# Scores of two heads at a time, with the high parts on two halves of the array's rows

## The chip, the core and the metric

The kernel runs on one core of a Trainium2 chip. The metric is the device time of one execution in microseconds (us). TensorE does the matrix products, VectorE (DVE) and ScalarE (ACT) the elementwise work, GpSimd (POOL) some small operations, and SyncE (SP) issues most of the transfers (DMA). PEld in the profile is TensorE's loading of the stationary operand ("weights"), which can overlap a running matmul. A matmul takes its stationary operand from SBUF as rows x columns, streams the moving operand through the array, and writes to PSUM, which the kernel uses as eight banks.

## The reference

Two layers of a decoder trunk on 512 positions of width 1024. Each layer is half a SwiGLU, a mixer, and another half SwiGLU. The mixer runs three kinds of attention from one input projection:

```python
for layer in range(DEPTH):                                   # DEPTH = 2
    x = x + 0.5 * swiglu(rmsnorm(x, g0), ...)
    x = x + hybrid_mixer(rmsnorm(x, g1), ...)
    x = x + 0.5 * swiglu(rmsnorm(x, g2), ...)

# in hybrid_mixer, heads of 64, causal, 512 positions
logits = einsum('bqhd,bsd->bqhs', qi, ki)                    # 8 index heads, one key
iscore = einsum('bqhs,bqh->bqs', relu(logits), wi)           # the top 128 keys of it are A's mask
sc_a = einsum('bqhd,bkd->bhqk', qa, ka) * scale              # 4 heads, one key head
sc_b = einsum('bqhd,bkhd->bhqk', qb, kb) * scale             # 4 heads
sc_c = einsum('bqhcd,bshcd->bhcqs', qc, kc) * scale          # 4 heads with 2 maps each
```

Each score goes through a masked softmax and is multiplied with the values.

## The kernel before

Values are float32. A product is kept exact enough by splitting each operand into a high part that the array takes in one pass (`F32R`) and a low part, the rest; `mm3` (L227 to L229) then makes a dense product of three passes (high x low, high x high, low x high).

Attention's scores use that a head has only 64 dimensions. `to_heads` splits the projected tile of a block of 128 positions into high and low (ACT at L819, DVE at L820), and the array transposes it head by head (L826), so that a head's tile has the 64 high rows on partitions 0 to 63 and the 64 low rows on 64 to 127. `swapped` makes a copy of a key tile with the halves exchanged, by two transfers from SP's queue. `scores` then takes two full passes for one head and one block `i` of 128 queries against the `(i + 1) * 128` keys so far: with the swapped keys (L844: high x low and low x high in one pass, the cross products), and with the keys as they are (L845: high x high and low x low). The moving operand is therefore 128, 256, 384 or 512 columns wide. The result goes to one of three PSUM banks with the tag `sc`, which the dense products of `product` use too.

Scores are made in `index_scores` (8 heads, i = 1 to 3), `attend` for B and for A (heads in pairs, i = 0 to 3; A has one key head for all) and `attend_c` (two maps of each head). Each is a generator. The loop at the end of `mixer` takes from it a step or two for each step of dense work (six dense matmuls, or a product), so that score passes stand in TensorE's queue between dense ones. `behind` ties them to the last dense matmul that was recorded, and a scheduler then settles the order. After the softmax, weights are transposed (L867) and multiplied with the values: L879 for C, and L892 in `weighted_pair` for A and B, which writes the two heads of a pair to the two halves of the output's partitions (so each matmul has 64 of the array's columns).

The feed-forward stages run before and after each mixer and contain no scores.

Of the kernel before, what the change touches and what calls it, by code (L numbers as in the profile page):

```python
# [13 lines left out]
F32 = mybir.dt.float32  # L14
# [3 lines left out]
AF = mybir.ActivationFunctionType  # L18
ALU = mybir.AluOpType
AX = mybir.AxisListType  # L20

P = 128
# [7 lines left out]
HD = 64  # L30
# [49 lines left out]
def trunk_kernel(ctx, tc, xt_in, pos_in, ng_in, wgu, wdn, wgrp, wgate, wbr_s, wbr_c, wo, qkg_in, lam_in, subg_in, out):  # L80
    nc = tc.nc
    V, S, G, PE = nc.vector, nc.scalar, nc.gpsimd, nc.tensor
# [12 lines left out]
    def nm(s):  # L95
        _n[0] += 1
        return f"{s}_{_n[0]}"

    def bank(tag="mm"):
        return ps.tile([P, 512], F32, tag=tag, name=nm(tag), bufs=BANKS[tag])  # L100

    def slot(dt=F32, tag="h", cols=512):
        return big.tile([P, cols], dt, tag=tag, name=nm(tag), bufs=SLOTS)

    def temp(tag, dt=F32, cols=512, bufs=2):
        return (phase[-1] if tag in ("p0", "p1", "pt", "e", "u") else tmp).tile([P, cols], dt, tag=tag, name=nm(tag), bufs=bufs)
# [622 lines left out]
    def mixer(l, n, nxt, aside):  # L729
# [71 lines left out]
        def defer(steps, fn):  # L801

            late.append([steps, fn])
# [9 lines left out]

        def to_heads(v, nh, t, dst, lag, done):

            s = phase[-1].tile([P, 8, 2, HD], F32R, tag="st", name=nm("st"), bufs=ST)

            def split():
                S.activation(s[:, :nh, 0, :], v[:, :nh], AF.Copy)  # L819
                V.tensor_tensor(s[:, :nh, 1, :], v[:, :nh], s[:, :nh, 0, :].bitcast(F32), op=ALU.subtract)  # L820
                defer(LAG_H, turn)

            def turn():
                ps_ = [bank("tr") for _ in range(0, nh, 4)]
                for h in range(nh):
                    PE.transpose(ps_[h // 4][:, h % 4 * P:(h % 4 + 1) * P].bitcast(F32R),  # L826
                                 s[:, h].rearrange("p a d -> p (a d)"), ident_r)
                for h in sorted(range(nh), key=lambda h: (h % 4, h)):
                    nc.any.tensor_copy(dst[h][:, t * P:(t + 1) * P], ps_[h // 4][:, h % 4 * P:(h % 4 + 1) * P])
                done[0] += 1  # L830

            defer(lag, split)

        def swapped(src):
            d = slot(F32R)
            nc.sync.dma_start(d[:HD, :].bitcast(F32), src[HD:, :].bitcast(F32))
            nc.sync.dma_start(d[HD:, :].bitcast(F32), src[:HD, :].bitcast(F32))
            return d

        def scores(q, k1, k2, i):  # L840

            o = bank("sc")[:, :(i + 1) * P]
            ql = q[:, i * P:(i + 1) * P]
            PE.matmul(o, ql, k2[:, :(i + 1) * P], start=True, stop=False)  # L844
            PE.matmul(o, ql, k1[:, :(i + 1) * P], start=False, stop=True)  # L845
            return o

        def softmax_parts(q, k1, k2, i, mask, tag):

            o = scores(q, k1, k2, i)  # L850
            w = (i + 1) * P
            mx = sm.tile([P, 1], F32, name=nm("mx"), tag="mx", bufs=4)
            pr = temp(tag, bufs={"p0": P0, "p1": P1}[tag])
            V.tensor_tensor_reduce(out=pr[:, :w], in0=o, in1=mask, scale=-1.0, scalar=-TAKEN,
                                   op0=ALU.add, op1=ALU.min, accum_out=mx)
            den = sm.tile([P, 1], F32, name=nm("den"), tag="den", bufs=4)
            S.activation(pr[:, :w], pr[:, :w], AF.Exp, scale=-1.0, bias=mx, accum_out=den)
            return pr, den
# [15 lines left out]
        def weighted(pr, i, v, then, lag):  # L874

            def values(pt):
                o = bank("tr")[:, :P]
                for j in range(i + 1):
                    PE.matmul(o, pt[:, j * P:(j + 1) * P], v(j), start=j == 0, stop=j == i)  # L879
                then(o)  # L880

            turned(pr, i, lambda pt: defer(LAG_V, lambda: values(pt)), lag)

        def weighted_pair(prs, i, vs, then, lag):

            pts = []

            def values():
                o = bank("tr")[:, :P]
                for j in range(i + 1):  # L890
                    for e in range(2):
                        PE.matmul(o[e * HD:(e + 1) * HD], vs[e](j), pts[e][:, j * P:(j + 1) * P], start=j == 0, stop=j == i)  # L892
                then(o)

            def collect(pt):
                pts.append(pt)
                if len(pts) == 2:
                    defer(LAG_V, values)

            for pr in prs:  # L900
                turned(pr, i, collect, lag)
# [4 lines left out]
        qis = [slot(F32R) for _ in range(8)]  # L906
        kis = [slot(F32R)]
# [61 lines left out]
        def causal_mask(i):  # L969
            return causal[:, 512 - (i + 1) * P:]  # L970
# [4 lines left out]
        def index_scores():  # L975
            ki2 = swapped(kis[0])
            for i in range(1, NT):
                w = (i + 1) * P
                acc = slot()
                for h in range(8):  # L980
                    o = scores(qis[h], kis[0], ki2, i)
                    r = temp("t2")
                    S.activation(r[:, :w], o, AF.Relu)
                    V.scalar_tensor_tensor(acc[:, :w], r[:, :w], wi[:, i, h:h + 1],
                                           causal[:, 512 - w:] if h == 0 else acc[:, :w], op0=ALU.mult, op1=ALU.add)
                    yield 1
                iscore.append(acc)
# [14 lines left out]
        def attend(name, qs, ks, k2s, mask, v, on):  # L1002

            for pair in range(2):
                heads = 2 * pair, 2 * pair + 1
                if k2s is None:
                    k2 = {h: swapped(ks[h]) for h in heads}
                else:
                    if not k2s:
                        k2s.append(swapped(ks[0]))  # L1010
                    k2 = {h: k2s[0] for h in heads}
                hi, lo = on[pair]
                for i in range(NT):
                    prs = []
                    for h in heads:
                        pr, den = softmax_parts(qs[h], ks[h], k2[h], i, mask(i), "p0")
                        rd = sm.tile([P, 1], F32, name=nm("rd"), tag="rd", bufs=4)
                        V.reciprocal(rd, den)
                        V.tensor_scalar(pr[:, :(i + 1) * P], pr[:, :(i + 1) * P], rd, None, op0=ALU.mult)
                        prs.append(pr)  # L1020
                        if h % 2 == 0:
                            yield 2

                    def split(o, hi=hi[:, i * P:(i + 1) * P], lo=lo[:, i * P:(i + 1) * P]):
                        S.activation(hi, o, AF.Copy)
                        V.tensor_tensor(lo, o, hi.bitcast(F32), op=ALU.subtract)
                        units[name] += 2

                    weighted_pair(prs, i, [lambda j, h=h: v(j, h) for h in heads], split, LAG_T)
                    yield 2  # L1030

        def attend_c(qs, ks, half, on):
            for hh in range(2):
                h = 2 * half + hh
                k2 = [swapped(ks[2 * hh]), swapped(ks[2 * hh + 1])]
                for i in range(NT):
                    w = (i + 1) * P
                    p0, d0 = softmax_parts(qs[2 * hh], ks[2 * hh], k2[0], i, causal_mask(i), "p0")
                    yield 2
                    p1, d1 = softmax_parts(qs[2 * hh + 1], ks[2 * hh + 1], k2[1], i, causal_mask(i), "p1")  # L1040
                    f = sm.tile([P, 1], F32, name=nm("f"), tag="f")
                    V.reciprocal(f, d1)
                    V.scalar_tensor_tensor(f, f, neg_lam[:, l:l + 1], d0, op0=ALU.mult, op1=ALU.mult)
                    r0 = sm.tile([P, 1], F32, name=nm("r0"), tag="r0", bufs=8)
                    V.reciprocal(r0, d0)
                    V.scalar_tensor_tensor(p0[:, :w], p1[:, :w], f, p0[:, :w], op0=ALU.mult, op1=ALU.add)
                    weighted(p0, i, lambda j, h=h: vc(j)[:, h * P:(h + 1) * P],
                             lambda o, to=on[hh][:, i * P:(i + 1) * P], r0=r0: sub_norm(o, to, r0), LAG_C)
                    yield 2
# [138 lines left out]
        for d in range(KD):  # L1188
# [5 lines left out]
            h, lo = slot(F32R), slot(F32R)  # L1194
# [4 lines left out]
        for d in range(KD):  # L1199
            x[d] = slot()  # L1200
            nc.sync.dma_start(x[d], aside[:, d, :])
            w = load_w(wo[l, d], WCOLS)
            o = bank()
# [77 lines left out]
```

## Time and profile before

| | |
|---|---|
| time, median of 3 runs | 2312.7 us (2312.01 to 2314.19) |
| profiled execution | 2315.78 us, span 2314.0 us |
| TensorE (PE) | 2286.2 us busy, 99% of the span, 13669 matmuls |
| weight loads (PEld) | 2013.8 us, 87% |
| DVE / ACT / POOL | 1721.5 us (74%) / 1117.9 us (48%) / 386.3 us (17%) |
| mean granted TensorE clock | 0.998 |

The span is the time from the first to the last instruction of the profiled execution; its own device time is a little longer. Busy shares are averages over the whole span. A matmul's recorded time includes its way through the array, so successive ones overlap in the record.

### The profile page before, as it was taken

The numbers are of one execution on the slowest core, as the hardware profiler recorded it, in microseconds if no ns is written. First come the engines' busy times: TensorE is split into PE (matmuls) and PEld (weight loads), VectorE is DVE, ScalarE is ACT, GpSimd is POOL, SyncE is SP. The second block draws the span as 40 slices with busy tenths as digits, with TensorE's granted clock in tenths as the row PEclk, the third lists the DMA queues.
The fourth block names the chain that finished last, engine by engine and source line by source line (L and its number), as shares of the span: only waits on it lengthen the run. The fifth ranks groups of instructions, "written<-read, shape, count | busy, mean of one in ns | idle before, by whom it ended". The sixth has DMA issues, their size and how long they took to land.

```text
span 2314.0 us, 36117 instructions
## 1 busy us (share of the span) xinstructions
PE 2286.2 (99%) x13669; PEld 2013.8 (87%) x13669; DVE 1721.5 (74%) x3126; ACT 1117.9 (48%) x2129; POOL 386.3 (17%) x509
## 2 busy tenths in 40 slices
PE   9999999999999999999999999999999999999999
PEld 7899988887878889999889999888888887899997
DVE  7777765788875778777687777647889666777774
ACT  5444435666433444444444444446764344544442
POOL 0111101455010111101011101024641110110100
PEclk9999999999999999999999999999999999999999
DMA  4665524323232456555256555232322224655551
GB/s 161 176 162 157 143 68 137 101 76 101 74 96 73 141 146 164 159 147 153 66 156 167 157 146 156 84 125 74 101 74 82 88 91 137 159 153 147 157 137 64
DMA packets 111646, 286.74 MB, mean 124 GB/s; under 512 B 13168, under 2 KB 13168, under 8 KB 111472
## 3 DMA queue, kind: packets, MB, share of 16 engines
q1 hardware_dynamic: 90016, 246.00, 33.6%
q0 software_dynamic: 20736, 37.76, 9.7%
q8 instruction: 107, 1.75, 0.3%
q10 hardware_dynamic: 720, 0.68, 0.1%
q14 instruction: 67, 0.55, 0.1%
HBM read 270.76 MB, written 6.29 MB: 120 GB/s over the span
## 4 chain that ended last, share of the span: by engine, by line
PE 85%; DVE 7%; DMA 3%; ACT 2%; issue 1%; POOL 1%; SPq 0%; ACTq 0%; DVEq 0%; POOLq 0%
PE mm L227 11%; PE mm L229 10%; PE mm L228 10%; PE sc L227 8%; PE sc L229 8%; PE sc L228 8%; PE tr L227 5%; PE tr L229 5%; PE tr L228 5%; PE mm L755 4%; PE mm L756 3%; PE mm L757 3%; DMA h<-h 1%; PE sc L844 1%; DVE lo L344 1%
## 5 line engine op out<-in xcount | busy, mean ns | idle before, releaser
L227 PE MATMUL mm<-h,hi 128*128 128x512 f32 x1216 | 481.9, 396 | 1.4 <-DVE h L547 0.8
L229 PE MATMUL mm<-h,lo 128*128 128x512 f32 x1216 | 475.4, 391 | 4.3 <-DVE lo L344 4.3
L228 PE MATMUL mm<-h,hi 128*128 128x512 f32 x1216 | 474.5, 390 | 0.0
L452 POOL DMA_DIRECT2D sa<-in_wgu x144 | 126.8, 1051 | 931.4 <-DMA sa<-in_wgu 428.8
L229 PEld LDWEIGHTS mm<-h,lo 128*128 128x128 f32 x1216 | 228.3, 188 | 54.9 <-DVE lo L344 6.1
L344 DVE TENSOR_TENSOR lo<-raw,hi 128x1024 fp32r<-128x1024 f32 (+1 forms) x198 | 232.9, 1179 | 57.7 <-ACT hi L341 57.0
L227 PEld LDWEIGHTS mm<-h,hi 128*128 128x128 f32 x1216 | 228.4, 188 | 48.8 <-issue 4.8
L227 PE MATMUL sc<-h,hi 128*128 128x256 f32 (+1 forms) x832 | 265.4, 319 | 0.0
L229 PE MATMUL sc<-h,lo 128*128 128x256 f32 (+1 forms) x832 | 264.3, 318 | 0.0
L228 PEld LDWEIGHTS mm<-h,hi 128*128 128x128 f32 x1216 | 228.6, 188 | 41.0
L228 PE MATMUL sc<-h,hi 128*128 128x256 f32 (+1 forms) x832 | 264.1, 317 | 0.0
L341 ACT ACTIVATE hi<-raw 128x1024 fp32r<-128x1024 f32 (+1 forms) x198 | 200.7, 1020 | 92.0 <-PE tr L228 58.1
L227 PE MATMUL tr<-h,hi 128*128 128x256 f32 (+1 forms) x704 | 214.1, 304 | 5.0 <-DVE h L283 5.0
L229 PE MATMUL tr<-h,lo 128*128 128x256 f32 (+1 forms) x704 | 213.7, 303 | 0.0
L228 PE MATMUL tr<-h,hi 128*128 128x256 f32 (+1 forms) x704 | 213.5, 303 | 0.0
L220 ACT ACTIVATE hi<-raw 128x1024 fp32r<-128x1024 f32 (+2 forms) x136 | 139.6, 1029 | 99.2 <-PE mm L228 66.7
L221 DVE TENSOR_TENSOR lo<-raw,hi 128x1024 fp32r<-128x1024 f32 (+2 forms) x136 | 173.3, 1276 | 17.1 <-ACT hi L220 16.2
L755 PE MATMUL mm<-hi,h 128*128 128x512 f32 (+2 forms) x448 | 172.4, 385 | 0.0
L227 PEld LDWEIGHTS sc<-h,hi 128*128 128x128 f32 x832 | 159.3, 191 | 12.8 <-issue 0.3
L228 PEld LDWEIGHTS sc<-h,hi 128*128 128x128 f32 x832 | 159.2, 191 | 12.1
L229 PEld LDWEIGHTS sc<-h,lo 128*128 128x128 f32 x832 | 159.2, 191 | 11.1 <-DVE lo L570 0.4
L757 PE MATMUL mm<-lo,h 128*128 128x512 f32 (+2 forms) x448 | 167.0, 373 | 0.0
(337 smaller groups left out, 5063.8 us busy)
## 6 DMA issues: line engine op xcount, KB each, us to landing
raw<-in_wgu SPq DMA_DIRECT2D x102, 512.0 KB, 4.8
sa<-in_wgu SPq DMA_DIRECT2D x72, 512.0 KB, 3.9
sa<-in_wgu POOLq DMA_DIRECT2D x144, 256.0 KB, 5.8
raw<-in_wdn SPq DMA_DIRECT2D x128, 256.0 KB, 4.7
raw<-in_wgate SPq DMA_DIRECT2D x48, 512.0 KB, 3.5
raw<-in_wgrp SPq DMA_DIRECT2D x40, 512.0 KB, 4.5
a<-in_wgu SPq DMA_DIRECT2D x72, 256.0 KB, 5.1
raw<-in_wdn SPq DMA_DIRECT2D x32, 384.0 KB, 3.5
```

The source lines that it names most:

```text
L220: S.activation(hi[:, sl], raw[:, sl], AF.Copy)
L221: V.tensor_tensor(lo[:, sl], raw[:, sl], hi[:, sl].bitcast(F32), op=ALU.subtract)
L227: PE.matmul(o, ah, bl, start=first, stop=False, skip_group_check=onto)
L228: PE.matmul(o, ah, bh, start=False, stop=False, skip_group_check=onto)
L229: last_mm[0] = PE.matmul(o, al, bh, start=False, stop=last, skip_group_check=onto)
L341: S.activation(self.h, self.src, AF.Copy)
L344: V.tensor_tensor(self.l, self.src, self.h.bitcast(F32), op=ALU.subtract)
L452: G.dma_start(self.sa[:, j * 512:(j + 1) * 512], src[:, 1536:], accum_op=ALU.add)
L755: PE.matmul(o[:, :w_cols], xl, wh[:, sl], start=k == 0, stop=False)
L756: PE.matmul(o[:, :w_cols], xh, wh[:, sl], start=False, stop=False)
L757: last_dense[0] = PE.matmul(o[:, :w_cols], xh, wl[:, sl], start=False, stop=k == KD - 1)
L844: PE.matmul(o, ql, k2[:, :(i + 1) * P], start=True, stop=False)
```

## The change

Two heads are handled by one call of `scores`, which takes two banks. It makes the full cross pass of each head, and then the product of the high parts of each head alone, as a matmul of 64 rows: rows 0 to 63 for the first head, 64 to 127 for the second. For that, `to_heads` puts the second head of each pair the other way round (low above high), by writing the split with other strides. The product low x low is no longer computed. With one key head for all (index scores and A) the keys and their swapped copy change places for the second head. The softmax of the second head still follows where it did.

```diff
         def to_heads(v, nh, t, dst, lag, done):
...
             def split():
-                S.activation(s[:, :nh, 0, :], v[:, :nh], AF.Copy)
-                V.tensor_tensor(s[:, :nh, 1, :], v[:, :nh], s[:, :nh, 0, :].bitcast(F32), op=ALU.subtract)
+                quads = s.rearrange("p (g e) a d -> p g (e a) d", e=2)
+                m_ = nh // 2
+                views = [(v[:, :2 * m_].rearrange("p (g e) d -> p g e d", e=2), quads[:, :m_, 0::3], quads[:, :m_, 1:3])]
+                if nh % 2:
+                    views.append((v[:, nh - 1], s[:, nh - 1, 0], s[:, nh - 1, 1]))
+                for x_, h_, l_ in views[nh == 1:]:
+                    S.activation(h_, x_, AF.Copy)
+                    V.tensor_tensor(l_, x_, h_.bitcast(F32), op=ALU.subtract)
                 defer(LAG_H, turn)
...
-        def scores(q, k1, k2, i):
-
-            o = bank("sc")[:, :(i + 1) * P]
-            ql = q[:, i * P:(i + 1) * P]
-            PE.matmul(o, ql, k2[:, :(i + 1) * P], start=True, stop=False)
-            PE.matmul(o, ql, k1[:, :(i + 1) * P], start=False, stop=True)
-            return o
-
-        def softmax_parts(q, k1, k2, i, mask, tag):
-
-            o = scores(q, k1, k2, i)
+        def scores(qs_, ks_, i):
+
+
+
+            w = (i + 1) * P
+            os_ = [bank("sc")[:, :w] for _ in range(2)]
+            ql = [q[:, i * P:(i + 1) * P] for q in qs_]
+            for o, q, (_, kx) in zip(os_, ql, ks_):
+                PE.matmul(o, q, kx[:, :w], start=True, stop=False)
+            for e, (o, q, (k, _)) in enumerate(zip(os_, ql, ks_)):
+                rows = slice(e * HD, (e + 1) * HD)
+                PE.matmul(o, q[rows], k[rows, :w], start=False, stop=True)
+            return os_
+
+        def softmax_parts(o, i, mask, tag):
+
             w = (i + 1) * P
...
                 for h in range(8):
-                    o = scores(qis[h], kis[0], ki2, i)
+                    if h % 2 == 0:
+                        os_ = scores(qis[h:h + 2], ((kis[0], ki2), (ki2, kis[0])), i)
                     r = temp("t2")
-                    S.activation(r[:, :w], o, AF.Relu)
+                    S.activation(r[:, :w], os_[h % 2], AF.Relu)
```

`attend` and `attend_c` call it in the same way, once for a pair of heads or maps. In the changed kernel the cross passes have the line L855, the half passes L858, the transposes of `to_heads` L833 and the matmuls of `weighted_pair` L904.

TensorE's queue in the first mixer, in the index scores at 384 columns, before (mm is a dense product, sc a score bank, h_4360 the swapped keys, h_3782 the keys, h_3774 and h_3775 two heads' queries):

```order
L757 MATMUL mm_4481<-lo_4289,h_3640 128x512
L844 MATMUL sc_4521<-h_4360,h_3774 128x384
L845 MATMUL sc_4521<-h_3782,h_3774 128x384
L755 MATMUL mm_4481<-hi_4294,h_3675 128x512
L756 MATMUL mm_4481<-hi_4294,h_3674 128x512
L757 MATMUL mm_4481<-lo_4295,h_3674 128x512
L755 MATMUL mm_4481<-hi_4294,h_3707 128x512
L756 MATMUL mm_4481<-hi_4294,h_3706 128x512
L757 MATMUL mm_4481<-lo_4295,h_3706 128x512
L844 MATMUL sc_4542<-h_4360,h_3775 128x384
L845 MATMUL sc_4542<-h_3782,h_3775 128x384
```

The same place in the changed kernel:

```order
L757 MATMUL mm_4484<-lo_4289,h_3640 128x512
L855 MATMUL sc_4521<-h_4360,h_3774 128x384
L855 MATMUL sc_4522<-h_3782,h_3775 128x384
L858 MATMUL sc_4521<-h_3782,h_3774 128x384
L858 MATMUL sc_4522<-h_4360,h_3775 128x384
L755 MATMUL mm_4484<-hi_4294,h_3675 128x512
```

The second head's passes moved up to those of the first, six dense matmuls earlier. 74 of the 88 pairs stand in this way. The other 14 are pulled apart by the scheduler, as at the first block of C's first maps, TensorE's queue in the first mixer of the changed kernel (tr_5306 and tr_5307 are transposes of `to_heads`, tr_5324 the output of a `weighted_pair`, h_5200 and h_5203 the swapped keys of the two maps):

```order
L757 MATMUL mm_5299<-lo_5277,h_3572 128x384
L855 MATMUL sc_5206<-h_5200,h_3789 128x128
L858 MATMUL sc_5206<-h_3793,h_3789 128x128
L833 MATMUL tr_5306<-ident_r,st_5057 128x128 x4
L833 MATMUL tr_5307<-ident_r,st_5057 128x128 x4
L904 MATMUL tr_5324<-pt_5240,h_3783 64x128
L904 MATMUL tr_5324<-pt_5247,h_3783 64x128
L904 MATMUL tr_5324<-pt_5240,h_3783 64x128
L855 MATMUL sc_5207<-h_5203,h_3790 128x128
L858 MATMUL sc_5207<-h_3794,h_3790 128x128
L904 MATMUL tr_5324<-pt_5247,h_3783 64x128
```

Here each half pass stands alone, and the second map's passes stand inside the block of 64-column matmuls, which was whole before; there are four such places. Before, the second map's passes stood behind the seventh of the transposes.

## Rows read from the trace of the kernel before

**Rows 1.** The chain that ended last, by engine, from the page.
```profile
PE 85%; DVE 7%; DMA 3%; ACT 2%; issue 1%; POOL 1%; SPq 0%; ACTq 0%; DVEq 0%; POOLq 0%
```

**Rows 2.** Busy time by stretch (the two mixers), as the header row says.
```profile
core 0: us, PE busy (x) PEld busy (x) DVE busy (x) ACT busy (x) POOL busy (x), PEclk, DMA share, GB/s
370.00:820.00 450.00, 444.62 (x2342) 370.34 (x2341) 334.37 (x784) 237.93 (x562) 126.27 (x177) 1.00 0.31 93
...
1510.00:1970.00 460.00, 454.54 (x2387) 378.56 (x2386) 340.85 (x796) 243.49 (x571) 127.74 (x179) 1.00 0.30 93
```

**Rows 3.** Groups of TensorE by line and shape: count, busy us, mean ns, idle.
```profile
L844 PE MATMUL sc<-h,h 128*128 128x512 f32 x48 | 19.2, 401 | 0.0
...
L844 PE MATMUL sc<-h,h 128*128 128x384 f32 x48 | 16.5, 344 | 0.0
...
L844 PE MATMUL sc<-h,h 128*128 128x256 f32 x48 | 13.7, 289 | 0.0
...
L844 PE MATMUL sc<-h,h 128*128 128x128 f32 x32 | 8.2, 261 | 4.1 <-DMA h<-h 4.1
```

**Rows 4.** Timeline of TensorE around score passes: start us, recorded us, line, shapes.
```profile
687.28 0.39 PE L844 MATMUL sc<-h,h 128*128 128x512 f32 x1
687.51 0.40 PE L845 MATMUL sc<-h,h 128*128 128x512 f32 x1
687.75 0.39 PE L227 MATMUL mm<-h,hi 128*128 128x512 f32 x1
...
696.72 0.22 PE L844 MATMUL sc<-h,h 128*128 128x128 f32 x1
...
696.89 0.45 PE L227 MATMUL mm<-h,hi 128*128 128x512 f32 x1
697.18 0.40 PE L228 MATMUL mm<-h,hi 128*128 128x512 f32 x1
...
706.14 0.28 PE L844 MATMUL sc<-h,h 128*128 128x256 f32 x1
706.25 0.28 PE L845 MATMUL sc<-h,h 128*128 128x256 f32 x1
706.37 0.40 PE L227 MATMUL mm<-h,hi 128*128 128x512 f32 x1
```

**Rows 5.** Timeline of TensorE around four transposes.
```profile
679.93 0.39 PE L229 MATMUL mm<-h,lo 128*128 128x512 f32 x1
680.16 0.60 PE L867 MATMUL tr<-ident,p 128*128 128x128 f32 x4
...
680.83 0.40 PE L228 MATMUL sc<-h,hi 128*128 128x512 f32 x1
```

**Rows 6.** Timeline of TensorE around blocks of eight and of four 64-column matmuls.
```profile
684.87 0.39 PE L229 MATMUL mm<-h,lo 128*128 128x512 f32 x1
685.19 0.66 PE L892 MATMUL tr<-pt,va 128*64 128x128 f32 x8
...
686.12 0.40 PE L228 MATMUL mm<-h,hi 128*128 128x512 f32 x1
...
710.77 0.39 PE L229 MATMUL mm<-h,lo 128*128 128x512 f32 x1
711.09 0.44 PE L892 MATMUL tr<-pt,va 128*64 128x128 f32 x4
...
711.80 0.39 PE L228 MATMUL mm<-h,hi 128*128 128x512 f32 x1
```

**Rows 7.** Timeline of the weight loads at the second block; in brackets, idle before.
```profile
710.55 0.19 PEld L229 LDWEIGHTS mm<-h,lo 128*128 128x128 f32 x1
711.09 0.20 PEld L892 LDWEIGHTS tr<-pt,va 128*64 128x64 f32 x4 [0.35 <-ACT p L857]
711.46 0.19 PEld L227 LDWEIGHTS mm<-h,hi 128*128 128x128 f32 x1 [0.17 <-issue]
```

**Rows 8.** Waits of TensorE over the span: us in total, times, longest us.
```profile
PE tr L227 <- DVE h L283: 5.0, 4, 2.0
...
PE sc L844 <- DMA h<-h: 4.1, 8, 0.9
```

More of the change, by code (lines that the diff above doesn't have):

```diff
@@ L1006, in attend @@
                 if k2s is None:
-                    k2 = {h: swapped(ks[h]) for h in heads}
+                    kp = [(ks[h], swapped(ks[h])) for h in heads]
                 else:
@@ L1010, in attend @@
                         k2s.append(swapped(ks[0]))
-                    k2 = {h: k2s[0] for h in heads}
+                    kp = [(ks[0], k2s[0]), (k2s[0], ks[0])]
                 hi, lo = on[pair]
@@ L1014, in attend @@
                     prs = []
+                    os_ = scores([qs[h] for h in heads], kp, i)
                     for h in heads:
-                        pr, den = softmax_parts(qs[h], ks[h], k2[h], i, mask(i), "p0")
+                        pr, den = softmax_parts(os_[h % 2], i, mask(i), "p0")
                         rd = sm.tile([P, 1], F32, name=nm("rd"), tag="rd", bufs=4)
@@ L1034, in attend_c @@
                 h = 2 * half + hh
-                k2 = [swapped(ks[2 * hh]), swapped(ks[2 * hh + 1])]
+                kp = [(ks[2 * hh + e], swapped(ks[2 * hh + e])) for e in range(2)]
                 for i in range(NT):
                     w = (i + 1) * P
-                    p0, d0 = softmax_parts(qs[2 * hh], ks[2 * hh], k2[0], i, causal_mask(i), "p0")
+                    os_ = scores(qs[2 * hh:2 * hh + 2], kp, i)
+                    p0, d0 = softmax_parts(os_[0], i, causal_mask(i), "p0")
                     yield 2
-                    p1, d1 = softmax_parts(qs[2 * hh + 1], ks[2 * hh + 1], k2[1], i, causal_mask(i), "p1")
+                    p1, d1 = softmax_parts(os_[1], i, causal_mask(i), "p1")
                     f = sm.tile([P, 1], F32, name=nm("f"), tag="f")
```

## The prediction

> **What bounds the kernel now.** I read the chain of work that ended last first [rows 1]: 85% of it is TensorE. The same holds inside the two stretches in which the changed lines run. By the table of stretches [rows 2] TensorE is busy 444.62 of 450 us in the first mixer and 454.54 of 460 in the second, DVE 334 and 341, and the granted clock is 1.00, the 2.4 GHz level. So TensorE has about 5.4 us to spare in each mixer, 11 us in all, and every other engine over 100 us. What the change does to TensorE's stream goes into the end almost one to one, and work that it adds to ACT or DVE does not. Only one wait of the score lines shows on TensorE: eight waits for the swapped copies, 4.1 us together [rows 8].
>
> **How long a full pass takes.** The recorded length of a matmul includes its way through the pipeline, so I go by start to start. At 512 columns a score pass follows the one before by 0.23 us, at 256 by 0.12 [rows 4]; for 384 I take 0.175, between them. At 128 columns I go by where the next stream can have begun: the second dense matmul of those rows starts at 697.18, one 0.23 us stream after the first really ran, so the two score passes took 696.72 to 696.95, 0.11 each. That is the time of a weight load: a block of four transposes, which lies between 679.93 + 0.23 and 680.83 - 0.23 by the same reasoning, takes 0.44 us, again 0.11 each, with nothing beside it [rows 5]. Calls by width are 32, 48, 48 and 48 for each of L844 and L845 [rows 3], and the rows of L845 repeat the counts. That makes 88 pairs of heads: 16, 24, 24 and 24. The two high-part passes of a pair cost 0.22, 0.24, 0.35 and 0.46 us today.
>
> **What the change does to these.** The cross passes stay. The 176 full high-part passes become 176 half-row passes, meant to run two at a time. The trace of before has no half-row matmul. The nearest thing in it is L892, whose output takes half of the array's columns, between full-array matmuls on both sides. Four of them take from 710.77 + 0.23 to 711.80 - 0.23, so 0.57 us; eight take from 684.87 + 0.23 to 686.12 - 0.23, so 0.79 us [rows 6]. So each costs 0.055 us, and there is a fixed 0.35 us per block that the transposes of [rows 5] don't have. The weight loads show where it lies [rows 7]: the load for L229 starts at 710.55, with the matmul before it, but the first of L892 only at 711.09, after L229's stream has ended (711.00), and the first full-array load behind the block sits idle 0.17 us and then delays its matmul. Nothing can be loaded ahead over the change of mode. Of the 0.35 us, 0.055 is the last small stream and 0.11 the first full load behind the block; some 0.185 is for emptying the array on the way in and out.
>
> The Trainium skill, "TensorEngine Tiling (Array Packing)", Key Properties, says that changing the tiling mode, not just the tile, drains TensorE. It lists the 64-row mode as one of the modes, and gives no price. The trace agrees for column halves; no run here shows row halves yet.
>
> I take the price of the column block for the row block. Lower bound: no fixed price (the first rival). Upper bound: the block price, and the two halves one after the other. I choose the block price because it is the only change of array mode in the trace, and it comes out alike in both blocks.
>
> **The sum.** A pair of halves that stands together costs 0.185 for emptying, three loads of 0.11 that nothing hides (the two halves' and the first full one behind), and the second half's stream: 0.57, 0.635, 0.69 and 0.745 us, against 0.22, 0.24, 0.35 and 0.46. That is 0.35, 0.395, 0.34 and 0.285 us more.
> In the built order 14 of the 88 pairs are not together (12 of 128 columns, 2 of 256), as the second order excerpt shows: each of their 28 halves enters and leaves the mode alone, for nothing, at 0.185 + 0.22 + its stream, so 0.46 or 0.525 instead of 0.11 or 0.12.
> - Whole pairs: 4 x 0.35 + 22 x 0.395 + 24 x 0.34 + 24 x 0.285 = 25.1 us.
> - Lone halves: 24 x 0.35 + 4 x 0.405 = 10.0 us.
> - Four of the lone halves cut a block of column halves in two (second excerpt), which adds at most the block's 0.35 us each: 1 us.
> - TensorE's idle 11 us can swallow a little, as engines that it waits for get more time: -2 us.
>
> **Costed at nothing.** The split into high and low parts in `to_heads` keeps its element counts; only the tile with five heads gets one more instruction on ACT and on DVE, 8 of each, under the 100 us that both have free per mixer. The second head's bank is filled two dense steps earlier and read when it was; behind a wait for it would stand all of TensorE's queue, but no such wait shows today and there are still three banks. The second head's swapped copy is needed earlier. Today's longest wait of that kind is 0.9 us [rows 8], so twelve places bound it at 11 us. I take 0, since the order puts that cross pass some five matmuls behind the first.
>
> The sum is +34 us. The profiled execution took 2315.78 us with a span of 2314.0, 3 us above the median of the runs; a difference carries over, so 2312.7 + 34 = 2347 us. Its own range is 2330 (the halves' loads side by side, 74 x 0.11 = 8 us less, and half of the emptying gone, 102 blocks x 0.09 = 9 us less) to 2357 (the halves one after the other, 74 streams of 0.15 on average, 11 us more).
>
> **Rivals.**
> *Faster: row halves need no change of mode.* Loads for the halves run ahead under the cross passes, and the two streams run side by side. A pair then saves one stream as far as the loads allow: 0.23 at 512, 0.175 at 384. At 256 four loads of 0.11 leave 0.04, or 0.12 with one load hidden ahead; I take 0.08. At 128 nothing. Sum: 24 x 0.23 + 24 x 0.175 + 22 x 0.08 = 11.5 us, so 2301. For it: halves of the rows lie on different partitions and banks. Against it: the fixed 0.35 us of [rows 6]. It decides if the fixed price per block is under 11.5 / 102 = 0.11 us.
> The Trainium skill, "TensorE: Matmul & The Clock Gate", Part 3, says that matmuls on different row groups run at once and that a load for a row group not in use is pulled ahead. It measured 3.07 times for four row tiles. Those are streams that stay in the mode, and no run here shows it.
> *No change: the halves run as ordinary passes.* No mode is entered and nothing runs side by side; a pass costs its stream whatever its rows. Then 176 passes stand for 176, and the time is 2313. Against it: L892 shows that half-array forms are treated apart.
> *Slower by another way: banks.* The pair takes two of three score banks at once, with `product` in the same rotation. If a pair waited 0.3 us for a bank each time, 88 x 0.3 = 26 us, so 2339. The table of waits, whose longest row stands in [rows 8] beside that of the score lines, has no row of a score pass that waits for DVE or ACT, so it is unlikely.
>
> **Numbers.** Forecast 0.68, faster rival 0.20, no change 0.09, banks 0.03. A measurement of this kernel tells about 0.2% (4.6 us) from no change. Faster 0.20, within 0.09, slower 0.71. The forecast's own range holds too little alone, so the range goes down to the faster rival: 2300 to 2355.
>
> **What would show it.** Right: half-row loads that begin only after the cross stream has ended; the first full load behind them late; 0.57 to 0.75 us per pair between the second cross pass's stream and the next dense one; mixer stretches longer by about 17 us each, the rest of the span unchanged. Wrong: half-row loads that start with the cross pass before them (then the faster rival), halves 0.23 us apart with no idle load (no change), or TensorE waiting for DVE or ACT at the first cross pass (banks).

## The result and the profile after

The changed kernel takes 2350.89 us (median of 6 runs, 2349.52 to 2352.61) against 2312.68: a ratio of 1.0166, with a 95% interval of 1.0153 to 1.0179. It is 38 us slower, where 34 were forecast, and inside the range.

The page of the kernel after, its first rows and the chain by engine:

```profile
span 2349.7 us, 36149 instructions
## 1 busy us (share of the span) xinstructions
PE 2318.8 (99%) x13669; PEld 2013.7 (86%) x13669; DVE 1723.4 (73%) x3126; ACT 1119.7 (48%) x2145; POOL 383.2 (16%) x509
...
PE 89%; DVE 5%; DMA 2%; ACT 1%; issue 1%; POOL 1%; SPq 0%; ACTq 0%; DVEq 0%; POOLq 0%
```

TensorE runs as many matmuls as before and holds more of the chain than the 85% of [rows 1]. The table of stretches, cut at about the same places of the program as [rows 2], with the stretch between the mixers:

```profile
core 0: us, PE busy (x) PEld busy (x) DVE busy (x) ACT busy (x) POOL busy (x), PEclk, DMA share, GB/s
...
370.00:840.00 470.00, 461.85 (x2340) 370.69 (x2340) 335.67 (x784) 239.14 (x571) 123.85 (x176) 0.99 0.29 89
840.00:1530.00 690.00, 686.46 (x4494) 629.98 (x4493) 525.14 (x764) 318.81 (x502) 68.07 (x76) 1.00 0.53 144
1530.00:2005.00 475.00, 468.98 (x2377) 377.14 (x2376) 338.27 (x790) 241.16 (x575) 124.85 (x177) 0.99 0.29 89
```

The first mixer is 20 us longer and the second 15; between them nothing moved. DVE and ACT have the same work as before. One thing was not in the forecast: the granted clock of the mixers is 0.99, where it was 1.00.

Now the score passes. First TensorE's timeline at a pair of 512 columns, then its weight loads at the same place (in brackets, idle before):

```profile
704.60 0.39 PE L229 MATMUL mm<-h,lo 128*128 128x512 f32 x1
704.82 0.63 PE L855 MATMUL sc<-h,h 128*128 128x512 f32 x2
705.38 0.50 PE L858 MATMUL sc<-h,h 64*128 64x512 f32 x2
705.81 0.50 PE L227 MATMUL mm<-h,hi 128*128 128x512 f32 x1
706.15 0.40 PE L228 MATMUL mm<-h,hi 128*128 128x512 f32 x1
```

```profile
704.60 0.41 PEld L855 LDWEIGHTS sc<-h,h 128*128 128x128 f32 x2
705.38 0.19 PEld L858 LDWEIGHTS sc<-h,h 64*128 64x128 f32 x2 [0.37 <-issue]
705.81 0.19 PEld L227 LDWEIGHTS mm<-h,hi 128*128 128x128 f32 x1 [0.24 <-issue]
```

Compare with [rows 6, 7]. The second cross stream ends at 704.82 + 0.46 = 705.28; the half-row loads begin only at 705.38, after 0.37 us of idleness on the load side; the first full load behind the halves comes after another 0.24. That is the emptying of the array on the way in and out that the column block showed. By the reasoning of the prediction the block lies between 704.60 + 0.23 and 706.15 - 0.23, 1.09 us. Without the two cross passes, 0.46, the halves cost 0.63, where the full passes cost 0.46 and the forecast said 0.745. The 0.11 too much stands in the second row: two loads take 0.19 us together, as long as one. The halves' loads run side by side too, not only their streams.

The rest of the 38 us lies at a few places in each mixer. Waits of TensorE in the kernel after (us in total, times, longest):

```profile
PE sc L855 <- DMA h<-h: 5.3, 5, 2.2
PE tr L227 <- DVE h L283: 5.0, 4, 2.2
...
PE tr L904 <- ACT pt L881: 4.2, 2, 2.3
...
PE sc L855 <- DVE mx L866: 1.0, 2, 0.8
```

Waits of about 2 us have come to the score stages. One is at a first block of C, in the timeline of ACT and then of TensorE:

```profile
526.42 0.56 ACT L826 ACTIVATE st<-t 128x256 fp32r<-128x256 f32 x2 [2.95 <-POOL t L772]
526.89 0.56 ACT L881 COPY pt<-tr 128x512 f32<-128x512 f32 x1
```

```profile
519.45 1.03 PE L879 MATMUL tr<-ident,p 128*128 128x128 f32 x8
...
524.93 0.32 PE L858 MATMUL sc<-h,h 64*128 64x128 f32 x1
527.51 1.44 PE L904 MATMUL tr<-pt,h 128*64 128x128 f32 x14 [2.25 <-ACT pt L881]
```

The transposes that the copy at 526.89 reads had ended by 520.5, but ACT did not take it before the split ahead of it in its queue. In the built order the second head's copy of transposed weights (`nc.any`, a copy whose engine is chosen when the kernel is recorded; L881) now stands on ACT behind a split for which POOL still turns the heads; before, both heads' copies stood ahead of that split. TensorE waits for it. What follows is in the table of stretches, around that wait:

```profile
526.00:528.20 2.20, 0.69 (x12) 0.69 (x13) 1.03 (x3) 1.75 (x7) 1.49 (x2) 0.98 1.02 400
528.20:533.50 5.30, 5.30 (x19) 3.57 (x16) 2.52 (x13) 1.97 (x9) 0.16 (x1) 0.50 0.09 34
```

TensorE is busy all the time in the second stretch, at a granted clock of 0.50, the 1.2 GHz level. The same pattern comes four times: a wait of 1.8 to 2.3 us (twice for a copy on ACT, twice for swapped keys), and 6.8 us at the lower level behind it.

The two waits for swapped keys stand at the first cross pass of a pair, so it is the first head's copy that is missing there. SP's queue and TensorE at the second pair of C's maps, in the first mixer:

```profile
557.65 0.47 SPq L843 DMA_DIRECT2D h<-h  x1
558.17 0.59 SPq L844 DMA_DIRECT2D h<-h  x1
558.85 0.55 SPq L843 DMA_DIRECT2D h<-h  x1
559.45 0.62 SPq L844 DMA_DIRECT2D h<-h  x1
...
562.89 0.30 PE L855 MATMUL sc<-h,h 128*128 128x128 f32 x1 [2.23 <-DMA h<-h]
...
564.59 0.22 PE L855 MATMUL sc<-h,h 128*128 128x128 f32 x1
```

The first two transfers make the first head's copy, and the pass at 562.89 waits for these two: by the trace's semaphores the second of them landed at 562.76. The second head's copy landed at 563.61, ahead of its pass at 564.59. In the kernel before, the same pair's copies were sent from 521.70 on and first used at 548.57:

```profile
521.70 0.47 SPq L836 DMA_DIRECT2D h<-h  x1
...
548.57 0.31 PE L844 MATMUL sc<-h,h 128*128 128x128 f32 x1
```

So 27 us between sending and first use became 5. Why the built order sends them so late here, no run shows.

### The profile page after: what moved, and what is told of

Same layout as the page of the kernel before. It is cut to its first block, busy times and chain, and to the rows that moved or that the text cites. A ratio compares the mean times of both kernels' runs of the same rounds, so it can differ in the third digit from the quotient of the medians.

```text
span 2349.7 us, 36149 instructions
## 1 busy us (share of the span) xinstructions
PE 2318.8 (99%) x13669; PEld 2013.7 (86%) x13669; DVE 1723.4 (73%) x3126; ACT 1119.7 (48%) x2145; POOL 383.2 (16%) x509
## 4 chain that ended last, share of the span: by engine, by line
PE 89%; DVE 5%; DMA 2%; ACT 1%; issue 1%; POOL 1%; SPq 0%; ACTq 0%; DVEq 0%; POOLq 0%
PE mm L227 11%; PE mm L229 11%; PE mm L228 11%; PE sc L227 8%; PE sc L229 8%; PE sc L228 8%; PE tr L227 5%; PE tr L229 5%; PE tr L228 5%; PE mm L755 4%; PE mm L757 4%; PE mm L756 3%; PE sc L858 1%; PE sc L855 1%; PE tr L904 1%
## 5 line engine op out<-in xcount | busy, mean ns | idle before, releaser
L755 PE MATMUL mm<-hi,h 128*128 128x512 f32 (+2 forms) x448 | 178.5, 398 | 0.0
L756 PE MATMUL mm<-hi,h 128*128 128x512 f32 (+2 forms) x448 | 168.2, 375 | 0.0
```

The costliest lines, as they stand in the source:

```text
L755: PE.matmul(o[:, :w_cols], xl, wh[:, sl], start=k == 0, stop=False)
L756: PE.matmul(o[:, :w_cols], xh, wh[:, sl], start=False, stop=False)
```

## The experiments

The change does two things at once: it enters another array mode, and it moves the second head's passes. The first four runs part them. My theory after the trace: the mode costs most of it, and waits at moved passes, with the clock behind them, the rest.

**Full passes at the new places.** One line differs from the changed kernel:

```diff
-                PE.matmul(o, q[rows], k[rows, :w], start=False, stop=True)
+                PE.matmul(o, q, k[:, :w], start=False, stop=True)
```

> The changed kernel with its order of instructions, but the two high-part passes of a pair are full 128-row passes again. Theory (the change of array mode costs most, the moved passes of the second head cost the rest): the trace after puts the mode at some 25 us and longer waits with their clock falls at some 13, so about 2326 us here. Rival, the mode costs nothing and all comes from moving the second head's passes: 2351. Rival, all of it is the mode: 2313.

Measured 2328.49 us, 1.0067 of the kernel before (1.0053 to 1.0080). So the mode is worth 2350.9 - 2328.5 = 22.4 us, and the moved passes 15.8. The long waits stand in this kernel's profile too, without a single half-row matmul:

```profile
PE sc L855 <- DMA h<-h: 6.1, 6, 2.2
...
PE tr L904 <- ACT pt L881: 4.0, 2, 2.0
PE sc L855 <- DVE mx L866: 2.2, 2, 1.7
```

**Half passes at the old places.** In the kernel before, one operand differs; low x low is left out:

```diff
-            PE.matmul(o, ql, k1[:, :(i + 1) * P], start=False, stop=True)
+            PE.matmul(o, ql[:HD], k1[:HD, :(i + 1) * P], start=False, stop=True)
```

> The kernel before, with its order, but each high-part pass takes only rows 0 to 63 (low x low is left out); nothing is paired or moved. Theory: each of 176 half passes enters and leaves the mode alone, at 0.29 us more for 32 of 128 columns and about 0.345 more for the other 144, 59 us: 2372 us. Rival, half-row passes are free and only the place of the second head's passes costs: 2313.

Measured 2369.24 us, 1.0244 (1.0230 to 1.0258): 57 us for 176 entries into the mode, 0.32 each net, though each half pass does half of the products. TensorE's timeline at 512 columns:

```profile
707.35 0.39 PE L229 MATMUL mm<-h,lo 128*128 128x512 f32 x1
707.58 0.40 PE L844 MATMUL sc<-h,h 128*128 128x512 f32 x1
707.91 0.50 PE L845 MATMUL sc<-h,h 64*128 64x512 f32 x1
708.34 0.50 PE L227 MATMUL mm<-h,hi 128*128 128x512 f32 x1
708.68 0.40 PE L228 MATMUL mm<-h,hi 128*128 128x512 f32 x1
```

From 707.35 + 0.23 to 708.68 - 0.23 are 0.87 us; less the cross pass 0.64. A lone half costs what two halves cost in the changed kernel (0.63). Its formula in the prediction, 0.185 + 0.22 + 0.23 = 0.635, holds at 512 columns. At 128 columns a lone half takes 0.40 instead of 0.46: the block of a cross pass and a half is 0.51 us long there, against 0.22 for the two full passes. Place by place a visit costs 0.29 us at 128 columns and 0.38 to 0.40 at the other widths, more than the 0.32 net; TensorE's idle time (span less busy time) fell from 27.8 us to 20.3 in the profiles, so some of the price went into time in which it had waited. The mean granted clock of this kernel was 0.999: half-row passes do not by themselves bring the clock down.

**Both halves on the same rows.** The changed kernel with high above low for every head:

```diff
-                rows = slice(e * HD, (e + 1) * HD)
+                rows = slice(0, HD)
```

The split in `to_heads` is again that of the kernel before, and keys and copy no longer change places for the second head.

> The changed kernel, but both heads keep high above low, so that both half passes of a pair use rows 0 to 63 and cannot run side by side. Theory, the two streams do run side by side in the changed kernel: each whole pair pays the second stream in full here, 0.23, 0.175, 0.12 and 0.1 us, some 13 us: about 2364 us. Rival, they never gained from each other: 2351.

Measured 2364.76 us, 1.0216 (1.0200 to 1.0232): 14 us over the changed kernel. Its timeline at 512 columns:

```profile
710.94 0.39 PE L229 MATMUL mm<-h,lo 128*128 128x512 f32 x1
711.16 0.63 PE L849 MATMUL sc<-h,h 128*128 128x512 f32 x2
711.72 0.73 PE L852 MATMUL sc<-h,h 64*128 64x512 f32 x2
712.38 0.50 PE L227 MATMUL mm<-h,hi 128*128 128x512 f32 x1
712.71 0.40 PE L228 MATMUL mm<-h,hi 128*128 128x512 f32 x1
```

The block is 1.31 us instead of 1.09, 0.22 more, which is one stream. So on different rows the two streams do run side by side, as the change means them to. It also shows what the price hangs on: a second half pass in the same visit adds its stream and not another 0.41 us, so the price is paid once for a visit to the mode and not by each half pass.

**First blocks as before.** For the first block of 128 queries, `attend` and `attend_c` make two full passes for each head when its turn comes (`scores_one` is the old `scores`):

```diff
-                    os_ = scores([qs[h] for h in heads], kp, i)
+                    os_ = scores([qs[h] for h in heads], kp, i) if i else None
                     for h in heads:
-                        pr, den = softmax_parts(os_[h % 2], i, mask(i), "p0")
+                        o_ = os_[h % 2] if i else scores_one(qs[h], kp[h % 2], i)
+                        pr, den = softmax_parts(o_, i, mask(i), "p0")
```

> The changed kernel, but for the first block of 128 queries in attend and attend_c each head makes two full passes where it did before the change; 72 pairs of 256 to 512 columns keep the halves. Theory: the waits of about 2 us at the first blocks and the clock falls behind them go, and so do the lone halves of 128 columns and the four cut blocks of column halves. Left are 24 pairs each at 0.27, 0.215 and 0.165 us, 16 us, and two lone halves more: about 2330 us. Rival, the waits come from pairs as such: 2340 or more.

Measured 2344.13 us, 1.0139 (1.0125 to 1.0153): the expectation missed by 14 us. The waits did not go, though the first blocks stand as before; its table of waits still has

```profile
PE sc L866 <- DMA h<-h: 5.1, 5, 1.8
...
PE tr L913 <- ACT pt L890: 3.7, 2, 2.4
```

L866 is here the cross pass of `scores_one`, in the place that it had before the change, and it still waits. So the waits do not need lone halves or paired first blocks. My next theory was that they hang on where the copy stands in ACT's queue, and on when the swapped keys are sent for. The next runs take these two causes away one after the other.

**The copy bound to DVE.** In the changed kernel, for the second head in `weighted_pair`:

```diff
-                nc.any.tensor_copy(pt[:, :w], p[:, :w])
+                (eng or nc.any).tensor_copy(pt[:, :w], p[:, :w])
...
-            for pr in prs:
-                turned(pr, i, collect, lag)
+            for e, pr in enumerate(prs):
+                turned(pr, i, collect, lag, V if e else None)
```

> The changed kernel, with the copy of the second head's transposed weights in weighted_pair bound to DVE instead of the engine that the recording picks. Theory: in the trace after this copy stands on ACT behind a split that waits for POOL, and TensorE waits 2.25 us for it in the first mixer and about 2 in the second, each with 6.8 us at the lower clock level behind it. Without it these two waits (4 us) and two of four clock falls (3.4 us each) go: about 2340 us. Rival, the clock falls come from the half-row mode and stay: 2347.

Measured 2342.91 us, 1.0133 (1.0118 to 1.0148): 8 us gained. The wait for the copy is gone from its table of waits, and in the mixers only the two clock falls behind the waits for swapped keys are left.

**Swapped keys sent for early as well.** On top of that, `attend` and `attend_c` issue the next pair's `swapped` in their third block when those heads are ready, as here in `attend_c` (`swap_ahead` keeps the copies until `swapped` asks for them):

```diff
+                    if i == 2:
+                        swap_ahead(*((f"c{half}", ks[2:4]) if hh == 0 else ("c1", kc1[:2] if half == 0 else [])))
```

> The same, and the swapped key copies of the next pair are issued from the third block of the pair before, when its heads are ready. Theory: the two waits of about 2 us for swapped copies go too, with the other two clock falls; what is left is the mode, 22 us by the run with full passes, a little less with 18 lone halves instead of 28: 2333 us. Rival, the pairs make other waits: 2340 or more.

Measured 2334.20 us, 1.0096 (1.0082 to 1.0111): another 9 us, to within 1 us of what the theory gave, though its six runs spread from 2329.5 to 2340.1. Its waits:

```profile
PE sc L866 <- DVE mx L877: 2.7, 2, 1.4
...
PE sc L866 <- DMA h<-h: 1.2, 3, 0.7
```

**The same with full passes.** Like that, with the one line of the first experiment.

> The same as e6_pin_early with full 128-row high-part passes: the order of pairs without the mode and without the four long waits. Theory: back at the kernel before, 2312 us (2309 to 2315). Rival, moving the second head's passes costs something else as well: 2318 or more.

Measured 2311.20 us, 0.9999 (0.9987 to 1.0010): the kernel before. The order of pairs costs nothing any more, and the halves at this order cost 2334.2 - 2311.2 = 23.0 us (by medians; the twelve runs with full passes lie between 2307.0 and 2317.5).

**The kernel before with early swaps alone.**

> The kernel before with the swapped copies issued early alone. Theory: its eight waits for the copies, 4.1 us, go: 2309 us. Rival, they move elsewhere: 2313.

Measured 2310.01 us, 0.9994 (0.9986 to 1.0003). Its waits for the copies fell from 4.1 us to 2.0. The interval holds 1, so this decides nothing; if something is won, it is less than the expected 4 us. No version tried here is faster than the kernel before beyond what the measurement can tell.

## Why the prediction held, and where it was off

**Place and sign: shown.** TensorE's stream went into the end almost one to one, only the mixers grew, and the price is the change of array mode: full passes in the same order are 22.4 us faster, lone halves in the old order 57 us slower, and a second half on the same rows adds no second price. This was read from the block of column halves [rows 6, 7]; the fixed price carried over to row halves. The Trainium skill's rule in "TensorEngine Tiling (Array Packing)", Key Properties, that a change of the tiling mode drains TensorE, agrees with the idle 0.37 and 0.24 us around the half-row loads here.

**The whole pairs: over-sized.** The step "three loads of 0.11 that nothing hides" counted the second half's load, which runs beside the first's (0.19 us for two). Without it a pair at 512 columns costs 0.185 + 0.22 + 0.23 = 0.635, measured 0.63. Over 74 pairs that is 8 us. The 36 us of the three terms on the mode become 28, against 22.4 measured. Most of the other 5 or 6 shows when the blocks are read place by place between dense passes of 512 columns, against the kernel with full passes: by medians a whole pair costs 0.27, 0.20 and 0.17 us more at 256, 384 and 512 columns (the mended formula says 0.285, 0.23 and 0.175), and a lone half of 128 columns 0.29 (the sum: 0.35). Over all pairs that is about 24 us; the rest is within the noise of two medians. At the order with early copies the mended formula gives 24.2 us (80 whole pairs, 16 lone halves) and the runs 23.0.

**The waits: missed.** "The second head's swapped copy is needed earlier ... I take 0" looked at the wrong copy. TensorE waited for the first head's, whose pass the change does not move; what had changed is when the transfers were sent, 5 us ahead of their first use instead of 27 at the pair shown above. The term says nothing of that, so it is by luck that its bound of 11 us comes near the size. And I put the edits of ACT and DVE at nothing by their spare time, without looking at where a copy on ACT would stand in its queue. Together these are the 15.8 us of the moved passes: binding the copy gave back 8.0, sending for the keys early 8.7, together 16.7, which the noise of these runs cannot tell from 15.8. Much of it is the clock behind the waits, since 6.8 us at half the rate lose 3.4 us of work: two waits of 2 us with their two falls come to 11 us by the trace, and 8.0 and 8.7 were given back for them.

The -2 us for idle time that swallows work did not come: TensorE's idle time rose from 27.8 to 30.9 us.

So the two errors, 14 us too much on the mode and 16 us missing on the waits, nearly cancelled. That the total came within 4 us is luck, and says nothing of its terms.

**Rivals.** Faster: its mechanism is right inside the mode (loads and streams of the halves run side by side, as the Trainium skill has it in "TensorE: Matmul & The Clock Gate", Part 3), but the price of getting there, some 0.4 us, is above the 0.11 at which it would win; at most one stream of 0.23 us is saved for it. No change: excluded by the lone halves. Banks: a wait for DVE at the cross passes exists (1.0 us in all after, up to 2.9 with early copies), far from 26.

## What to carry to other kernels

Before packing small matmuls on parts of the array, count how often TensorE would change mode, and look for any matmul in the trace that uses part of the array: the time from the last full stream before such a block to the first behind it, less the streams, is the price per visit, and a visit must save more than that. When code moves work of one engine, look at the built order of the other engines too: which copy now stands behind which wait, and when each transfer is issued against its new use. A wait of TensorE can cost more than its length, so read the granted clock of the stretch behind it.

## What the runs showed of the hardware

- Two weight loads for different row halves take 0.19 us together, as one does; for the same rows 0.29 (the loads of L858 above, and here those of the kernel with both halves on the same rows):

```profile
711.72 0.29 PEld L852 LDWEIGHTS sc<-h,h 64*128 64x128 f32 x2 [0.36 <-issue]
```

- TensorE's granted clock fell to 0.50 for 6.8 us after each of the four waits of 1.8 to 2.3 us in the mixers of the changed kernel. In the kernel before, whose longest waits in the mixers' score passes are 0.9 us [rows 8], no score pass has such a fall behind it. But the length of one wait does not settle it. The 1.00 of the second mixer [rows 2] is rounded and hides a fall of 3.4 us at 1967, behind a wait of 1.2 us for DVE (L283); in the changed kernel the same wait is 1.2 us long too, and no fall follows.
